# A two-layer hybrid encoder: the squares of the MLP norm taken unit by unit, one weight pool for all phases, and MLP weights prepared during the output projection

## Chip, cores and metric

One Trainium2 chip, one core, one launch. The metric is the device time of a run in microseconds (us); the median of three runs counts. A profile is one execution seen by the hardware profiler.

## The reference, cut to what matters

The input is 512 tokens of 1024 features; 16 learned tokens are put in front (L = 528). Two layers follow, each an attention block and an MLP, each behind an RMS norm, everything in float32:

```python
for layer in range(DEPTH):                       # DEPTH = 2
    u = rmsnorm(h, attn_norm_g[layer])
    mix = ab_mixer(...) if layer % 2 == 0 else c_mixer(...)   # both end in an output projection
    h = h + mix
    u = rmsnorm(h, mlp_norm_g[layer])            # u * rsqrt(mean(u*u) + 1e-6) * g
    h = h + square(relu(u @ w_ff1[layer])) @ w_ff2[layer]     # 1024 -> 4096 -> 1024
return h[:, N_META:]
```

The square of the ReLU lets the norm's factor be taken out: `r2` = 1 / (mean(h*h) + eps) is multiplied onto the MLP's result instead of onto its input.

## The kernel before, in words

Features lie on the 128 partitions, tokens along the free axis; `hk[m]` (m = 0 to 7) is the residual of feature tile m, 128 x 528. A float32 product is made of three reduced-precision ones: weights and activations are each split into a high part (a cast on ScalarE: `wh`, `ah`, `xh`) and a low part (a subtraction on VectorE: `wl`, `al`, `xl`), and the matmuls wh·xh, wh·xl, wl·xh are accumulated. `load_unit` (L213) loads a unit of weights with a transfer on SP's queue, casts it (L221) and subtracts (L222); `gemm` (L225, matmuls at L232) multiplies. One unit is 8 x 128 x 128 weights, 512 KB, and at 528 tokens 48 matmuls.

The program runs through phases: attention of layer 0 (AB), its output projection (O0), MLP 0 (M0), attention of layer 1 (C), its projection (O1, in two halves of the contraction), MLP 1 (M1). In layer 1 the MLP works on the last 512 tokens. The order of the attention phases is written out by hand (`ORDER`, `ORDER_C`); within it, and everywhere else, a planner at build time places the instructions of each engine by program order and by its own estimate of when operands and buffers are free. Buffers come from pools stacked at the left or the right of SBUF. A pool that is closed gives its memory to the next one, and a tile there waits for the tiles that lay in the same place. The weights of each phase have a pool of their own, opened by `weight_pool(name)`, which closes the one before (L155).

Output projection, layer 0 (L1159): for m = 0 to 7, load `hr` (the input tile) on SP's queue, multiply, add into `hk[m]` (L1164), `park(0, m)` it to device memory on POOL's queue (L1152), and call `fast.add(m)` (L1106). The last prepares the operands for the first MLP product, which is done with seven products of half size where eight would be needed (a Strassen-like scheme over two halves of the features and of the tokens). Tiles 0 to 3 need few operations ("light" in what follows: one cast, two splits); tiles 4 to 7 ("heavy") make the combinations T2, T3, T4 with tile m - 4. In O1 the same is done at L1510.

MLP (`mlp`, L1174): four quarters q of 1024 hidden features. In a quarter, four `pair` calls make 16 weight groups' worth of products (L1250, 336 matmuls), then eight units of the second weight matrix follow (L1318, 48 matmuls each, or 24 of double width in layer 1), whose results are gathered in `hk[m]`. `weight_groups` (L1196) prepares the groups one after the other: for a pair of first-matrix units it makes the four sums of half units with one add over 1024 elements (L1226) and two over 512 (L1228, L1230), then casts (L1201) and subtracts (L1202). `prepare` keeps a ring of five groups ahead of the products. The MLP's weight pool is opened when the MLP begins (L1177), on the left, where the temporaries of `fast` and the projection's weights were.

Sum of squares: after the products of quarter 1, `sum_squares` (L1136) reloads the eight parked tiles on POOL's queue (L1191, two `hr` buffers), squares each on ScalarE (L1143) and adds on VectorE (L1146). A matmul with the constant `onesd` (L1313) sums over the features, L1315 adds eps, L1316 takes the reciprocal `r2`. It is first used in quarter 2 (L1331).

Of the kernel before, what the change touches and what calls it, by code (L numbers as in the profile page):

```python
# [17 lines left out]
P = 128  # L18
D = 1024
KT = D // P  # L20
# [114 lines left out]
def build(tc, ins, out, dbg=None):  # L135
# [13 lines left out]
    cst = ctx.enter_context(tc.tile_pool(name="cst", bufs=1, side="left"))  # L149
    xp = ctx.enter_context(tc.tile_pool(name="xp", bufs=1, side="left"))  # L150
    dp = ctx.enter_context(tc.tile_pool(name="dp", bufs=1, space=DRAM))

    wpool = {}

    def weight_pool(name, bufs=2):  # L155

        if "cm" in wpool:
            wpool.pop("cm").__exit__(None, None, None)
        if name is not None:
            wpool["cm"] = tc.tile_pool(name=name, bufs=bufs, side="left", reuse_waits="tile")  # L160
            wpool["p"] = wpool["cm"].__enter__()
        return wpool["p"]

    weight_pool("wab")
# [48 lines left out]
    def load_unit(src):  # L213

        k, m = src.shape[1], src.shape[2]
        wp = wpool["p"]
# [824 lines left out]
    weight_pool(None)  # L1041
# [94 lines left out]
    def sum_squares(pool, src, tags=("sqk", "sqa")):  # L1136

        sq = None
        for k in range(KT):
            s = pool.tile([P, L], F32, name="sqk", tag=tags[0], bufs=2)  # L1140
            x = src(k)
            t0 = L - x.shape[1]
            S.activation(out=s[:, t0:], in_=x, func=AF.Square)  # L1143
            if k:
                t = pool.tile([P, L], F32, name="sqa", tag=tags[1], bufs=2)
                V.tensor_tensor(out=t[:, t0:], in0=sq[:, t0:], in1=s[:, t0:], op=ALU.add)  # L1146
                s = t
            sq = s
        return sq
# [3 lines left out]

    fq_cm = tc.tile_pool(name="fq0", bufs=1, side="left", reuse_waits="tile")
    fq = fq_cm.__enter__()
    ft_cm = tc.tile_pool(name="ft0", bufs=1, side="left", reuse_waits="tile")
    fast = Fast(fq, ft_cm.__enter__(), PK_G + 8, 0)
    weight_pool("wo0")
    for m in range(KT):  # L1159
# [7 lines left out]
    weight_pool(None)  # L1167
    ft_cm.__exit__(None, None, None)
    yp_cm.__exit__(None, None, None)
    tap("h1", h)  # L1170

    RING = 5

    def mlp(layer, t0, fast, final):  # L1174
        lp_cm = tc.tile_pool(name=f"mlp{layer}", bufs=1, side="right", reuse_waits="tile")
        lp = lp_cm.__enter__()
        wp = weight_pool(f"wm{layer}")  # L1177
# [15 lines left out]

        def weight_groups():  # L1196
            def split(src):
                k = src.shape[1]
                wh = wp.tile([P, KT, P], F32R, name="wh", tag="wh", bufs=RING)
                wl = wp.tile([P, KT, P], F32R, name="wl", tag="wl", bufs=RING)  # L1200
                S.copy(out=wh[:, :k], in_=src)  # L1201
                V.tensor_tensor(out=wl[:, :k], in0=src, in1=wh[:, :k], op=ALU.subtract)  # L1202
                return wh, wl

            def load(name, i):
                raw = wp.tile([P, 4, 4, P], F32, name="raw", tag="raw", bufs=2)
                for j in range(2):
                    nc.sync.dma_start(out=raw[:, 2 * j:2 * j + 2].rearrange("p a k m -> p (a k) m"),
                                      in_=ins[f"{name}_{layer}"][i + j])
                return raw  # L1210

            flat = lambda t: t.rearrange("p a k m -> p (a k) m")
            todo = [(w, q * 8 + m) for q in range(4) for w in ("w1", "w2") for m in range(0, 8, 2)]
            loaded = [load(*todo[0])]
            for i, (w, m) in enumerate(todo):
                if i + 1 < len(todo):
                    loaded.append(load(*todo[i + 1]))
                raw = loaded.pop(0)
                if w == "w2":
                    yield split(flat(raw[:, 0:2]))  # L1220
                    yield split(flat(raw[:, 2:4]))
                    continue
                s = wp.tile([P, 4, 4, P], F32, name="sums", tag="sums", bufs=1)
                yield split(flat(raw[:, 0:2]))
                wide4 = lambda t: t.rearrange("p a k m -> p a (k m)")
                V.tensor_tensor(out=wide4(s[:, 1:3]), in0=wide4(raw)[:, 0:4:3],  # L1226
                                in1=wide4(raw[:, 2:3]).to_broadcast([P, 2, 4 * P]), op=ALU.add)
                V.tensor_tensor(out=s[:, 3], in0=s[:, 2], in1=raw[:, 0], op=ALU.add)  # L1228
                yield split(flat(s[:, 2:4]))
                V.tensor_tensor(out=s[:, 0], in0=s[:, 3], in1=raw[:, 1], op=ALU.add)  # L1230
                yield split(flat(s[:, 0:2]))
                yield split(raw[:, 3])

        source = weight_groups()
        groups, used = [], set()

        def prepare():

            while len(groups) < RING or len(groups) - RING in used:
# [377 lines left out]
```

## Time and profile before

| | |
|---|---|
| median of 3 runs | 1378.26 us (1375.27 to 1379.09) |
| the profiled execution | 1378.83 us, span 1377.1 us |
| mean granted clock of TensorE | 0.967 of 2.4 GHz |
| VectorE, ScalarE, POOL busy | 67%, 51%, 8% of the span |
| DMA queues, share of 16 engines | SP's 22.7%, POOL's 2.9% |

The span is the time from the first to the last instruction. A matmul's record overlaps its neighbours', so a busy TensorE is not one at its peak; where it stands idle, the views name what ended the wait. Times within the span are us from its start. PEclk is the granted clock of TensorE as a share of 2.4 GHz; 0.5 means that it ran at 1.2 GHz.

### The profile page before, as it was taken

Reading aid. Unit: us, or ns where it says so; the run is one execution under the profiler, and the core shown is the slowest. Engines: PE = TensorE matmul, PEld = TensorE weight load, DVE = VectorE, ACT = ScalarE, POOL = GpSimd, SP = SyncE. Lnnn points to the kernel's source line nnn. Section 1 sums busy time; section 2 is a strip of 40 time slices with the busy share of each in tenths; the row PEclk is TensorE's granted clock in tenths of the full one; section 3 lists DMA queues with packets and bytes.
Section 4 is the critical chain, followed back from the end, with each engine's and each line's share of the span. In section 5 each row is a group of like instructions: output and inputs, shape, how many; then the busy total and the mean of one; then the engine's idle time right before and its main releaser. Section 6 shows DMA issues by size and latency. Waiting matters only on the chain.

```text
span 1377.1 us, 22737 instructions
## 1 busy us (share of the span) xinstructions
PE 1288.0 (94%) x8979; PEld 1188.1 (86%) x8979; DVE 921.8 (67%) x1847; ACT 702.0 (51%) x1412; POOL 113.7 (8%) x250
## 2 busy tenths in 40 slices
PE   7989998999879999599999999999989995999998
PEld 6988998888779999599999988888779894898996
DVE  6687769785568537547677468698786384476762
ACT  4634655566436538217347166675566372173460
POOL 1060505210010000100000000000100001000000
PEclk9998999999898999799999999999989997999999
DMA  4321211000453414312424011101334133124241
GB/s 165 108 62 31 63 32 47 1 2 14 142 158 106 138 47 134 113 63 92 154 78 168 32 47 47 44 19 34 127 138 148 61 128 117 62 95 151 78 138 46
DMA packets 35930, 118.08 MB, mean 86 GB/s; under 512 B 4456, under 2 KB 4584, under 8 KB 35696
## 3 DMA queue, kind: packets, MB, share of 16 engines
q1 hardware_dynamic: 31984, 103.86, 22.7%
q0 software_dynamic: 3840, 12.78, 2.9%
q8 instruction: 70, 1.15, 0.3%
q14 instruction: 36, 0.29, 0.1%
HBM read 110.25 MB, written 6.37 MB: 85 GB/s over the span
## 4 chain that ended last, share of the span: by engine, by line
PE 63%; issue 24%; DVE 5%; ACT 4%; POOL 2%; DMA 2%; SPq 0%; POOLq 0%; ACTq 0%; DVEq 0%
PE dn L232 28%; PE dn L1250 12%; PE cq L232 5%; PE po L1495 2%; PE dn L1468 2%; DMA hr<-hdram 1%; PE pw L1489 1%; PE pw L993 1%; POOL u L647 1%; DVE cy L442 1%; PE rw L695 1%; POOL ut L646 1%; PE rw L681 1%; PE rw L748 1%; PE rw L736 1%
## 5 line engine op out<-in xcount | busy, mean ns | idle before, releaser
L232 PE MATMUL dn<-ah,wh 128*128 128x264 f32 (+1 forms) x896 | 234.5, 320 | 4.9 <-ACT wh L221 4.9
L232 PE MATMUL dn<-ah,wl 128*128 128x264 f32 (+1 forms) x896 | 232.3, 318 | 0.6 <-DVE wl L222 0.6
L232 PE MATMUL dn<-al,wh 128*128 128x264 f32 (+1 forms) x896 | 231.3, 316 | 0.0
L1201 ACT CAST wh<-raw 128x1024 fp32r<-128x1024 f32 (+1 forms) x128 | 120.5, 943 | 201.1 <-PE dn L232 172.1
L1202 DVE TENSOR_TENSOR wl<-raw,wh 128x1024 fp32r<-128x1024 f32 (+1 forms) x128 | 139.3, 1090 | 63.9 <-ACT wh L1201 62.2
L232 PEld LDWEIGHTS dn<-ah,wh 128*128 128x128 f32 x896 | 149.6, 191 | 16.2 <-ACT wh L221 5.1
L1250 PE MATMUL dn<-xh,wh 128*128 128x264 f32 (+1 forms) x512 | 152.6, 298 | 11.7 <-ACT wh L1201 10.9
L232 PEld LDWEIGHTS dn<-al,wh 128*128 128x128 f32 x896 | 149.6, 191 | 12.0 <-issue 0.5
L232 PEld LDWEIGHTS dn<-ah,wl 128*128 128x128 f32 x896 | 148.6, 190 | 11.8 <-DVE wl L222 0.9
L1250 PE MATMUL dn<-xh,wl 128*128 128x264 f32 (+1 forms) x512 | 146.8, 289 | 1.6 <-DVE wl L1202 1.6
L1250 PE MATMUL dn<-xl,wh 128*128 128x264 f32 (+1 forms) x512 | 147.2, 288 | 0.0
L1250 PEld LDWEIGHTS dn<-xh,wh 128*128 128x128 f32 x512 | 99.2, 194 | 18.1 <-ACT wh L1201 12.1
L1202 DVE TENSOR_TENSOR wl<-sums,wh 128x1024 fp32r<-128x1024 f32 x64 | 78.0, 1224 | 39.4 <-ACT wh L1201 38.8
L1201 ACT CAST wh<-sums 128x1024 fp32r<-128x1024 f32 x64 | 66.8, 1050 | 72.4 <-PE dn L232 45.2
L1250 PEld LDWEIGHTS dn<-xh,wl 128*128 128x128 f32 x512 | 98.9, 194 | 2.5 <-DVE wl L1202 2.5
L1250 PEld LDWEIGHTS dn<-xl,wh 128*128 128x128 f32 x512 | 99.4, 194 | 0.1
L221 ACT CAST wh<-raw 128x1024 fp32r<-128x1024 f32 (+1 forms) x58 | 54.0, 932 | 88.2 <-PE dn L232 48.1
L232 PE MATMUL dn<-xh,wh 128*128 128x264 f32 x416 | 91.5, 297 | 1.1 <-DVE last L1335 0.8
L232 PE MATMUL dn<-xl,wh 128*128 128x264 f32 x416 | 90.4, 293 | 0.0
L232 PE MATMUL dn<-xh,wl 128*128 128x264 f32 x416 | 89.2, 293 | 0.0
L1328 DVE TENSOR_TENSOR h<-h,dn 128x528 f32<-128x528 f32 (+1 forms) x32 | 22.3, 696 | 76.3 <-PE dn L232 76.3
L222 DVE TENSOR_TENSOR wl<-raw,wh 128x1024 fp32r<-128x1024 f32 (+1 forms) x58 | 63.0, 1088 | 11.6 <-ACT wh L221 11.1
(507 smaller groups left out, 2978.5 us busy)
## 6 DMA issues: line engine op xcount, KB each, us to landing
raw<-in_w SPq DMA_DIRECT2D x128, 512.0 KB, 4.3
raw<-in_w_in SPq DMA_DIRECT2D x22, 512.0 KB, 3.6
raw<-in_w_c SPq DMA_DIRECT2D x12, 512.0 KB, 3.6
hr<-hdram POOLq DMA_DIRECT2D x16, 264.0 KB, 3.0
raw<-in_w_o SPq DMA_DIRECT2D x8, 512.0 KB, 4.5
raw<-in_w_o SPq DMA_DIRECT2D x16, 256.0 KB, 2.6
hr<-hdram POOLq DMA_DIRECT2D x16, 256.0 KB, 2.9
gcb<-gdram SPq DMA_DIRECT2D x8, 264.0 KB, 4.4
```

What stands on the lines that cost most here:

```text
L221: S.copy(out=wh, in_=raw)
L222: V.tensor_tensor(out=wl, in0=raw, in1=wh, op=ALU.subtract)
L232: T.matmul(o, a[:, k, :], b[k][:, sl], start=first and k == 0 and i == 0, stop=last and k == n - 1 and i == 2)
L442: V.scalar_tensor_tensor(out=y[:, a:a + n], in0=x[:, b:b + n], scalar=w(j), in1=y[:, a:a + n], op0=ALU.mult, op1=ALU.add)
L646: G.tensor_tensor(out=ut[:, :, :, :n], in0=arow, in1=ucol, op=ALU.mult)
L647: G.tensor_tensor(out=udst, in0=udst, in1=ut[:, :, :, :n], op=ALU.subtract)
L1201: S.copy(out=wh[:, :k], in_=src)
L1202: V.tensor_tensor(out=wl[:, :k], in0=src, in1=wh[:, :k], op=ALU.subtract)
L1250: T.matmul(o, a[:, half * 4 + k, :], b, start=start and k == 0 and i == 0, stop=k == 3 and i == 2, skip_group_check=not start)
L1328: V.tensor_tensor(out=tview(ak), in0=tview(ak), in1=pview(ps), op=ALU.add)
L1468: T.matmul(ps[:, s, :HL], a[:, sl], b[:, s * HL:(s + 1) * HL], start=i == 0, stop=i == 2)
L1495: T.matmul(po, a[:, kc, :], b, start=kc == 0 and i == 0, stop=kc == NC and i == 2)
```

## The change

1. `sum_squares` now handles one tile. In the MLP it is called in each of the eight units of quarter 0, behind the copy of the unit's result, and adds into one tile `sq`; after quarter 1's products only the `onesd` matmul, L1315 and L1316 are left. The statistics of layer 1's attention call it eight times in a row.
2. One weight pool `wp` (two buffers each of raw, high and low parts) is opened at the start, below the other left pools, and kept to the end; `load_unit` takes its buffers in all phases. The MLP gets a further pool, `wm0` or `wm1` (raw 2, high 3, low 3, sums 1), and its groups and raw tiles go in turn to this one and to `wp`.
3. The preparing of groups becomes a class `Weights` that is made before the output projection's last part. After every second tile of O0 and of the second half of O1, `prepare` is called with limits of 1, 2 and 3 groups, and after the eighth without one (so to five).
4. The projections take the tiles in the order 0, 4, 1, 5, 2, 6, 3, 7.
5. The four sums of a pair are four adds of 512 elements each, and the first pair loads the next one's units after its third group instead of at once.
6. `yp` is closed before the temporaries of `fast`, which move to the right side.

```diff
     cst = ctx.enter_context(tc.tile_pool(name="cst", bufs=1, side="left"))
+    wp = ctx.enter_context(tc.tile_pool(name="wp", bufs=2, side="left"))
     xp = ctx.enter_context(tc.tile_pool(name="xp", bufs=1, side="left"))
...
-    weight_pool("wab")
...
+    def sum_squares(pool, k, sq, x, tag="sqk"):
+        t0 = L - x.shape[1]
+        if k == 0:
+            S.activation(out=sq[:, t0:], in_=x, func=AF.Square)
+            return
+        s = pool.tile([P, L], F32, name="sqk", tag=tag, bufs=2)
+        S.activation(out=s[:, t0:], in_=x, func=AF.Square)
+        V.tensor_tensor(out=sq[:, t0:], in0=sq[:, t0:], in1=s[:, t0:], op=ALU.add)
...
+    RING = 5
+    class Weights:
+        def __init__(self, layer, pool):
+            self.layer, self.pool = layer, pool
+            self.groups, self.used, self.raws = [], set(), 0
+            self.source = self.produce()
+        def place(self, n, size, kind, dtype):
+            pool, bufs = (self.pool, size - 2) if n % size < size - 2 else (wp, 2)
+            return pool.tile([P, KT, P], dtype, name=kind, tag=kind, bufs=bufs)
+        def load(self, w, m):
+            o = []
+            for i in (m, m + 1):
+                o.append(self.place(self.raws, 4, "raw", F32))
+                self.raws += 1
+                nc.sync.dma_start(out=o[-1], in_=ins[f"{w}_{self.layer}"][i])
+            return o
+        def split(self, src):
+            k, n = src.shape[1], len(self.groups)
+            wh, wl = (self.place(n, RING, kind, F32R) for kind in ("wh", "wl"))
+            S.copy(out=wh[:, :k], in_=src)
+            V.tensor_tensor(out=wl[:, :k], in0=src, in1=wh[:, :k], op=ALU.subtract)
+            self.groups.append((wh, wl))
+        def produce(self):
+            todo = [(w, q * 8 + m) for q in range(4) for w in ("w1", "w2") for m in range(0, 8, 2)]
+            loaded = [self.load(*todo[0])]
+            for i, (w, m) in enumerate(todo):
+                ahead = lambda: loaded.append(self.load(*todo[i + 1])) if i + 1 < len(todo) else None
+                if i:
+                    ahead()
+                u0, u1 = loaded.pop(0)
+                if w == "w2":
+                    yield self.split(u0)
+                    yield self.split(u1)
+                    continue
+                s = self.pool.tile([P, 4, 4, P], F32, name="sums", tag="sums")
+                yield self.split(u0)
+                V.tensor_tensor(out=s[:, 2], in0=u1[:, :4], in1=u1[:, 4:], op=ALU.add)
+                V.tensor_tensor(out=s[:, 3], in0=s[:, 2], in1=u0[:, :4], op=ALU.add)
+                yield self.split(s[:, 2:4].rearrange("p a k m -> p (a k) m"))
+                V.tensor_tensor(out=s[:, 0], in0=s[:, 3], in1=u0[:, 4:], op=ALU.add)
+                V.tensor_tensor(out=s[:, 1], in0=u0[:, :4], in1=u1[:, :4], op=ALU.add)
+                yield self.split(s[:, 0:2].rearrange("p a k m -> p (a k) m"))
+                if not i:
+                    ahead()
+                yield self.split(u1[:, 4:])
+        def prepare(self, limit=None):
+            while len(self.groups) < RING or len(self.groups) - RING in self.used:
+                if limit is not None and len(self.groups) >= limit or next(self.source, self) is self:
+                    return
+
     fq_cm = tc.tile_pool(name="fq0", bufs=1, side="left", reuse_waits="tile")
     fq = fq_cm.__enter__()
-    ft_cm = tc.tile_pool(name="ft0", bufs=1, side="left", reuse_waits="tile")
+    wm_cm = tc.tile_pool(name="wm0", bufs=1, side="left", reuse_waits="tile")
+    weights = Weights(0, wm_cm.__enter__())
+    yp_cm.__exit__(None, None, None)
+    ft_cm = tc.tile_pool(name="ft0", bufs=1, side="right", reuse_waits="tile")
     fast = Fast(fq, ft_cm.__enter__(), PK_G + 8, 0)
-    weight_pool("wo0")
-    for m in range(KT):
+    MIXED = (0, 4, 1, 5, 2, 6, 3, 7)
+    for i, m in enumerate(MIXED):
...
         park(0, m)
         fast.add(m)
+        if i % 2:
+            weights.prepare((i + 1) // 2 if i < 7 else None)
...
             if q == 1:
-                sq = sum_squares(lp, reload, ("c0", "c1"))
                 ps = ps_dense()
...
                 if q == 0:
                     S.copy(out=tview(ak), in_=pview(ps))
+                    sum_squares(lp, m, sq, reload(m), "c0")
...
-        for m in range(KT):
+        for i, m in enumerate(MIXED):
             mark("O1")
-            ps = ps1("cq") if k0 == 0 else ps1(("cq", "po")[m % 2])
+            ps = ps1("cq") if k0 == 0 else ps1(("cq", "po")[i % 2])
...
                 fast.add(m)
+                if i % 2:
+                    weights.prepare((i + 1) // 2 if i < 7 else None)
...
+    wm_cm = tc.tile_pool(name="wm1", bufs=1, side="left", reuse_waits="tile")
+    weights = Weights(1, wm_cm.__enter__())
     weave((c_out(4, KT), 1))
```

## Rows read from the trace of the kernel before

**Rows 1.** The page's first part: busy us of each engine, its share of the span, its instructions.
```profile
PE 1288.0 (94%) x8979; PEld 1188.1 (86%) x8979; DVE 921.8 (67%) x1847; ACT 702.0 (51%) x1412; POOL 113.7 (8%) x250
```

**Rows 2.** The view of waits, TensorE's own: waiting tile and line, what released it, us in total, times, longest.
```profile
PE dn L1313 <- DVE sqa L1146: 33.6, 2, 16.9
PE dn L1250 <- ACT wh L1201: 10.9, 3, 6.5
...
PE dn L232 <- ACT wh L221: 4.9, 1, 4.9
PE po L232 <- DVE wl L222: 3.2, 1, 3.2
```

**Rows 3.** The timeline of POOL, ScalarE, VectorE and TensorE around the sum of squares of layer 0: start, duration (us), engine, line, operation, operands, count, and in brackets the idle time before and what ended it. One tile of the eight, and the matmul at the end.
```profile
557.05 0.55 POOL L1191 DMA_DIRECT2D hr<-hdram  x1 [1.48 <-ACT sqk L1143]
...
560.00 0.65 ACT L1143 ACTIVATE sqk<-hr 128x528 f32<-128x528 f32 x1 [1.42 <-DMA hr<-hdram]
...
560.68 0.71 DVE L1146 TENSOR_TENSOR sqa<-sqa,sqk 128x528 f32<-128x528 f32 x1 [1.35 <-ACT sqk L1143]
...
565.35 2.13 PE L1313 MATMUL dn<-sqa,onesd 128*128 128x264 f32 x4 [16.88 <-DVE sqa L1146]
```

**Rows 4.** The chain that ended last, in order of time: start, us, what. L232 here are the unit stages of the MLPs, L1250 their product stages, L1313 the `onesd` matmul of layer 1's MLP, L1362 the same four matmuls in layer 1's attention statistics.
```profile
615.65 42.60 PE dn L1250 x336
658.24 46.30 PE dn L232 x384
...
804.15 1.16 PE dn L1362 x4
...
1152.57 2.07 PE dn L1313 x2
...
1200.87 41.53 PE dn L1250 x336
1242.40 44.18 PE dn L232 x192
```

**Rows 5.** The groups of instructions by line: line, engine, operation, operands, count, busy us, mean ns of one, idle before and its releasers.
```profile
L1202 DVE TENSOR_TENSOR wl<-sums,wh 128x1024 fp32r<-128x1024 f32 x64 | 78.0, 1224 | 39.4 <-ACT wh L1201 38.8 <-PE dn L1250 0.5
...
L1226 DVE TENSOR_TENSOR sums<-raw 128x1024 f32<-128x1024 f32 x32 | 39.0, 1220 | 0.8 <-DMA raw<-in_w 0.6
...
L1230 DVE TENSOR_TENSOR sums<-sums,raw 128x512 f32<-128x512 f32 x32 | 22.1, 692 | 1.0
...
L1146 DVE TENSOR_TENSOR sqa<-sqa,sqk 128x528 f32<-128x528 f32 (+1 forms) x18 | 12.6, 703 | 15.1 <-ACT sqk L1143 14.7
...
L1143 ACT ACTIVATE sqk<-hr 128x528 f32<-128x528 f32 (+1 forms) x16 | 10.2, 638 | 15.9 <-DMA hr<-hdram 13.2 <-DVE sqa L1146 2.7
```

**Rows 6.** The timeline from O0 to M0, SP's queue and TensorE (columns as in rows 3): the first MLP loads, the last projection matmuls, the first product, the first product record of 0.28 us, the start of the unit stage.
```profile
406.30 3.44 SPq L1208 DMA_DIRECT2D raw<-in_w  x4
...
404.13 0.41 PE L232 MATMUL dn<-ah,wl 128*128 128x264 f32 x2
410.99 0.59 PE L1250 MATMUL dn<-xh,wh 128*128 128x264 f32 x1 [6.45 <-ACT wh L1201]
...
421.30 0.28 PE L1250 MATMUL dn<-xh,wh 128*128 128x264 f32 x1
...
459.51 0.41 PE L232 MATMUL dn<-ah,wh 128*128 128x264 f32 x2
```

**Rows 7.** Windows: from:to, length, then for PE, PEld, DVE, ACT and POOL busy us (instructions), granted clock, DMA share, GB/s. The first is O1, the second O0, the third the end of the attention of layer 0, the fourth the end of O1.
```profile
976.00:1003.70 27.70, 21.24 (x87) 16.36 (x85) 24.31 (x53) 17.53 (x34) 5.41 (x10) 0.90 0.58 192
353.20:404.50 51.30, 49.52 (x384) 49.04 (x384) 30.22 (x51) 19.74 (x33) 4.54 (x8) 0.94 0.46 136
300.00:349.50 49.50, 46.98 (x358) 41.67 (x356) 27.89 (x86) 31.81 (x105) 1.83 (x13) 1.00 0.10 33
992.00:1003.70 11.70, 5.24 (x18) 3.36 (x16) 10.63 (x26) 6.26 (x12) 1.62 (x3) 0.76 0.58 205
```

**Rows 8.** TensorE's timeline from O1 to M1: the second tile's first matmul, the wait for a low part in the last tile, the first product, the start of the unit stage.
```profile
976.40 0.39 PE L232 MATMUL po<-ah,wh 128*128 128x512 f32 x1
...
996.88 0.50 PE L232 MATMUL po<-ah,wl 128*128 128x512 f32 x1 [3.22 <-DVE wl L222]
...
1003.75 0.58 PE L1250 MATMUL dn<-xh,wh 128*128 128x256 f32 x1 [3.29 <-ACT wh L1201]
...
1050.08 0.40 PE L232 MATMUL dn<-ah,wh 128*128 128x512 f32 x1
```

**Rows 9.** Timelines of SP's queue, POOL, ScalarE, VectorE and TensorE at the start of O0: the last attention weights and the first projection weights loaded, a reload of quarter 1 issued in O0, the first activation casts, the weight casts, the last low parts of the activations, the first projection matmul.
```profile
211.17 0.33 SPq L220 DMA_DIRECT2D raw<-in_w_in  x1
...
342.49 0.33 SPq L220 DMA_DIRECT2D raw<-in_w_o  x1
...
400.31 0.55 POOL L1191 DMA_DIRECT2D hr<-hdram  x1
...
348.99 2.22 ACT L1067 CAST ah<-yA 128x528 fp32r<-128x528 f32 x4
...
353.25 1.99 ACT L221 CAST wh<-raw 128x1024 fp32r<-128x1024 f32 x2
...
352.48 2.56 DVE L1068 TENSOR_TENSOR al<-yB,ah 128x528 fp32r<-128x528 f32 x4
...
354.34 0.81 PE L232 MATMUL dn<-ah,wh 128*128 128x264 f32 x2 [4.88 <-ACT wh L221]
```

More of the change, by code (lines that the diff above doesn't have):

```diff
@@ L149, in build @@
     cst = ctx.enter_context(tc.tile_pool(name="cst", bufs=1, side="left"))
+    wp = ctx.enter_context(tc.tile_pool(name="wp", bufs=2, side="left"))
     xp = ctx.enter_context(tc.tile_pool(name="xp", bufs=1, side="left"))
     dp = ctx.enter_context(tc.tile_pool(name="dp", bufs=1, space=DRAM))
[L153 to L162, printed above, removed]
-    weight_pool("wab")
     psum = {}
@@ L215, in load_unit @@
         k, m = src.shape[1], src.shape[2]
-        wp = wpool["p"]
         raw = wp.tile([P, k, m], F32, name="raw", tag="raw")
@@ L1040, in build @@
     ab_cm.__exit__(None, None, None)
-    weight_pool(None)
     psum_pool("psm0", dn=4)
@@ L1134, in add @@
             self.split("T4", i, *part("T4"), t4, -1.0)
[L1136 to L1149, printed above, removed]
+    def sum_squares(pool, k, sq, x, tag="sqk"):
[6 more added lines that the diff above has]
+        V.tensor_tensor(out=sq[:, t0:], in0=sq[:, t0:], in1=s[:, t0:], op=ALU.add)
@@ L1166, in build, with mlp @@
         fast.add(m)
-    weight_pool(None)
+        if i % 2:
+            weights.prepare((i + 1) // 2 if i < 7 else None)
     ft_cm.__exit__(None, None, None)
-    yp_cm.__exit__(None, None, None)
     tap("h1", h)
-    RING = 5
-    def mlp(layer, t0, fast, final):
+    def mlp(layer, t0, fast, weights, final):
         lp_cm = tc.tile_pool(name=f"mlp{layer}", bufs=1, side="right", reuse_waits="tile")
         lp = lp_cm.__enter__()
-        wp = weight_pool(f"wm{layer}")
+        groups, used, prepare = weights.groups, weights.used, weights.prepare
         n = fast.n
@@ L1192, in reload @@
             return o
[L1196 to L1239, printed above, removed]
-                g = next(source, None)
-                if g is None:
-                    return
-                groups.append(g)
         def product(o, g, half, name, start):
@@ L1301, in mlp @@
         r2, base = None, 0
+        sq = lp.tile([P, L], F32, name="sqa")
         for q in range(4):
@@ L1341, in build @@
     xs2 = []
-    mlp(0, 0, fast, lambda m: xs2.append(make_x(m, PK_G + 16)))
-    weight_pool(None)
+    mlp(0, 0, fast, weights, lambda m: xs2.append(make_x(m, PK_G + 16)))
+    wm_cm.__exit__(None, None, None)
     fq_cm.__exit__(None, None, None)
@@ L1350, in build @@
     psum_pool("psc", dn=2, pw=2, po=1, cq=1)
-    weight_pool("wc")
     cp_cm = tc.tile_pool(name="cp", bufs=1, side="right", reuse_waits="tile")
@@ L1358, in stats @@
     def stats():
-        sq = sum_squares(cp, lambda k: hk[k])
+        sq = cp.tile([P, L], F32, name="sqa", tag="sqa")
+        for k in range(KT):
+            sum_squares(cp, k, sq, hk[k])
         ps = ps_dense()
@@ L1529, in build @@
     fast = Fast(fq, ft_cm.__enter__(), PK_G + 24, NM)
+    wm_cm = tc.tile_pool(name="wm1", bufs=1, side="left", reuse_waits="tile")
+    weights = Weights(1, wm_cm.__enter__())
     weave((c_out(4, KT), 1))
     ft_cm.__exit__(None, None, None)
-    weight_pool(None)
     tap("h3", h)
@@ L1536, in build @@
     mark("M1")
-    mlp(1, NM, fast, lambda m: nc.sync.dma_start(out=out[m], in_=hk[m][:, NM:]))
-    weight_pool(None)
+    mlp(1, NM, fast, weights, lambda m: nc.sync.dma_start(out=out[m], in_=hk[m][:, NM:]))
+    wm_cm.__exit__(None, None, None)
     fq_cm.__exit__(None, None, None)
```

## The prediction

> **What bounds the kernel now.** I read the page's busy times first: TensorE is busy for 94% of the span [rows 1], so a gain must come from the stretches where it stands still or runs at its lower clock. The view of waits on TensorE lists them: of the larger ones, one line takes 33.6 us in two waits, the `onesd` matmul of L1313 behind the sum of squares; then come three waits of the first MLP products for their prepared weights (10.9 us), the first output projection waiting for its weight cast (4.9), and an output-projection product of layer 1 waiting for VectorE (3.2) [rows 2]. The timeline around the first long wait shows why it lasts: a reload is issued only when the square before last has freed one of two `hr` buffers, the square waits for the transfer, the add for the square, about 1.9 us a tile, and TensorE starts after the eighth [rows 3]. All four kinds of wait are touched by the change.
>
> **Sum of squares: the price per layer.** TensorE did its last product before the wait at 565.35 - 16.88 = 548.47 us [rows 3], and the unit stage of that quarter ended where the next products begin, at 615.65: 67.2 us. The same stage of the next quarter, without the wait, takes 46.30 us [rows 4]. What stays between is the `onesd` matmul alone; the same four matmuls of the layer-1 statistics, at full clock, take 1.16 us [rows 4]. So the stage becomes 46.30 + 1.16 = 47.5 and 19.7 us go. Layer 1: the wait is 33.6 - 16.9 = 16.7 us and ended at 1152.57, the stage at 1200.87: 1200.87 - (1152.57 - 16.7) = 65.0 us; the next quarter takes 44.18; with 1.1 us for the matmul 45.3, and 19.7 us go [rows 2, 4]. Both include the lower clock after the wait. Together **39.4 us**. What is late next is the reciprocal for `r2`, but it stays behind the same matmul on VectorE as before and its first user is a quarter later.
>
> The work moves into the eight units of the first quarter: per unit one reload on POOL's queue, one square (0.64 us on ScalarE) and one add (0.70 on VectorE) [rows 5]. A unit lasts 46.30/8 = 5.8 us on TensorE [rows 4], in which VectorE and ScalarE otherwise do about one weight split and one copy, so I cost it at nothing. The square stands on ScalarE behind the unit's PSUM copy and in front of the next group's cast; five groups are ready ahead, so a late reload would have to last several units before TensorE sees it. Uncovered it would cost 8 x (0.64 + 0.70) = 10.7 us a layer. The layer-1 attention statistics use the same helper with the same counts: nothing.
>
> **Sums of the first weights.** One add of 1024 elements (1220 ns) and two of 512 (692) become four of 512: 0.16 us more for each of 32 pairs, 5 us of VectorE in all [rows 5]. In the steady quarters VectorE has room, so nothing; 5 us if that cover were gone.
>
> **First weights in layer 0.** Today the loads for the MLP begin at 406.30, after the last projection matmul (404.13 + 0.41 = 404.54); the first product starts at 410.99, and the clock is back at the rate of 0.28 us per record only at 421.30. The unit stage begins at 459.51 [rows 6]. A stage of the same 336 matmuls takes 42.60 us when nothing is late [rows 4], so 459.51 - 404.54 - 42.60 = 12.4 us are lost. In the change groups 0 to 2 are ready inside the projection. That brings forward about 4 x 0.69 of sums and 4 x 1.22 + 0.68 of low parts, 8.4 us of VectorE (five groups), into a stage where it is busy 30.2 of 51.3 us [rows 5, 7]: it fits. The reordering 0, 4, 1, 5, ... matters here because a light tile (0 to 3) then follows each heavy one. The last tile, 7, is last in both orders, and its operands come 2 to 3 us after its matmul, while the first product (tiles 0 to 3 only) and three quarters of the second cover them. Groups 3 and 4 lie in the shared buffers and are split only after tile 7; group 4 is wanted after 60 products, about 7.3 us after the projection, and I expect it at 7. I take **10 us** of the 12.4, bounds 6 and 12.4.
>
> **First weights of the output projection, layer 0.** The pool kept through the phases has free raw, high and low buffers long before the projection: the last attention weights were issued at 211.17, the first projection weights only at 342.49, and their casts stand behind the eight activation casts, so TensorE begins at 354.34 after 4.88 us [rows 9]. The planner does move independent work far ahead: it issued a reload of the second quarter at 400.31 [rows 9], inside the projection, because its buffer was free. If it does so here, the two casts leave the start of the stage; TensorE is then paced by the low parts of the activations, which end at 352.48 + 2.56 = 355.0 [rows 9], and the first tile ends near 355.6 instead of about 404.5 - 7 x 5.8 = 364 (5.8 us being a unit of as many matmuls, 46.30/8 [rows 4]). Bounds: 0 (the casts stay) and 8; I take **5**, nearer to the upper one, since the moved reload is the nearest row. On the way the casts cost 2 x 2.3 us of ScalarE and VectorE in the attention stage, where TensorE is busy 47.0 of 49.5 us [rows 7]: bounds 0 and 4.5, I take 0.
>
> **First weights in layer 1.** Here VectorE is already the limit: 24.3 of 27.7 us from 976 on, 10.63 of the last 11.7 [rows 7]; TensorE waits 3.22 us for it before 996.88, waits 3.29 for the first weight cast before 1003.75, and the unit stage begins at 1050.08 [rows 8]. The second tile begins at 976.40 [rows 8]; seven tiles of 12 matmuls (44.18/16 = 2.76 us each) and a product stage of 41.53 [rows 4] would end at 976.4 + 19.3 + 41.5 = 1037.2, so 12.9 us are lost. But VectorE's work for the tiles has to be done before the second product can end, and groups 0 to 2 now add 4 x 0.69 + 3 x 1.22 = 6.4 us in front of tile 7. The 24.3 us of tile work plus 6.4, less some 2 for the last operands of tile 7 that are wanted later, end near 1006 if VectorE never idles, say 1006 to 1009; of the products, 336 - 21 then remain, 38.9 us: 1045 to 1048 before any slow clock. I take **2 us**, bounds -2 and +9 (the upper one if the groups can be prepared before the projection, which needs their memory to be free while the attention runs).
>
> **Sum.** 39.4 + 10 + 5 + 2 = 56.4. The rows come from one execution of 1378.8 us (span 1377.1, 1.7 around it), 0.6 above the median of the three runs, so nothing has to be shifted: 1378.8 - 56.4 = **1322 us**.
>
> **Rivals.** *Only the sum of squares pays* (15%): the early weights don't come early, because the loads' memory is held by the attention's tiles or VectorE is full, and what is won at the start of the MLP was lost in the projection. For it: layer 1's rows above. Against it: VectorE's 21 idle us in layer 0. 1378.8 - 39.4 = 1339, with the layer-0 bound 1333 to 1341.
> *All of it pays* (17%): 39.4 + 12.4 + 8 + 9 = 68.8, 1310 us. For it: the planner's reach. Against it: groups 3 and 4 come last, layer 1's VectorE.
> *The squares get in the way* (3%): the reload or the square of each unit holds ScalarE and the ring runs dry; with the uncovered 10.7 us in both layers the forecast becomes 1322 + 21 = 1343. Against it: the five groups ahead.
> *Slower* (2%): in the reordered projections VectorE is late once in every pair of tiles, and TensorE never gets back to 2.4 GHz. The stretch with the wait of 3.22 us was granted 0.76 [rows 7], and after the wait of 6.45 us the records stayed longer than 0.28 us, at 1.2 GHz, from 410.99 to 421.30 [rows 6]. In layer 1, at half the clock, the 96 projection matmuls and the 336 products would take up to twice as long, 22 + 41.5 = 64 us more, against 39.4 won: 1403 us. It decides from 39.4 + 17 us on, so only when nearly all of both stages runs at the lower clock. Against it: a stage limited by VectorE hides much of a slower TensorE.
> The Trainium skill, TensorE: Matmul & The Clock Gate, section HAM oscillation — how this bites in real kernels, says that a wait which returns in each pass of a loop drops the clock in each pass, so that the price is paid again and again instead of once. By that rule the last rival would be the forecast for layer 1; the trace agrees as far as single waits go (the 0.76 above), and no row shows waits that return.
>
> **How the numbers follow.** The forecast has 60%, the rest is small mixtures of these. Its own range is 1315 to 1330 from the bounds of its terms. The range for 8 in 10 takes in the case in which all pays and most of that in which only the sum of squares does: 1307 to 1341. About 0.3% (4 us) is what a measurement of this kernel can tell from no change; of the cases only the slower one and a sliver of the mixtures reach it, so faster 0.96, the same 0.01, slower 0.03.
>
> **What would show it.** Right: no wait of TensorE at the `onesd` matmul and a second-quarter unit stage near 47.5 and 45.3 us; squares one per unit in the first quarter; in layer 0 the unit stage beginning some 43 to 46 us after the last projection matmul; the first projection casts before the activation casts. In layer 1 I expect TensorE's waits for VectorE inside the projection to grow and those after it to shrink. Wrong: a wait at `onesd` that is still several us, waits of the units in the first quarter, or a projection stage of layer 0 clearly longer than 8 x 5.8 us.

## The result, and the profile after

The changed kernel takes 1324.27 us (median of four runs, 1323.57 to 1325.03), the kernel before beside it 1378.67 (1375.27 to 1380.79): a ratio of 0.9608, 95% interval 0.9587 to 0.9628. The forecast was 1322. The span went from 1377.1 to 1322.8 us, 54.3 less. On the page TensorE is now busy for 97% of it instead of 94 [rows 1], and its mean granted clock is 0.988 instead of 0.967.

The busy times of the page, and TensorE's longer waits (what waited, for what, us in total, times, longest):

```profile
PE 1279.5 (97%) x8979; PEld 1181.8 (89%) x8979; DVE 917.9 (69%) x1879; ACT 699.3 (53%) x1412; POOL 114.5 (9%) x250
```

```profile
PE cq L220 <- DVE h L1508: 4.2, 2, 2.7
PE dn L1246 <- DVE wl L1167: 3.3, 2, 1.9
...
PE dn L1360 <- DVE sqa L1131: 1.4, 1, 1.4
```

Of the four kinds of wait in [rows 2] only the last has a successor of its size: in O1 TensorE now waits 4.2 us for the adds into `h`. The 33.6 us at the `onesd` matmul (now L1309) are gone.

The chain that ended last (start, us, what) has the stages in order. L220 are the units of 48 matmuls (before: L232), L1246 the products (before: L1250); the lines answer to [rows 4]:

```profile
442.55 46.33 PE dn L220 x384
...
579.04 42.78 PE dn L1246 x336
621.83 46.31 PE dn L220 x384
...
1014.37 44.16 PE dn L220 x192
...
1145.67 42.01 PE dn L1246 x336
1187.69 44.14 PE dn L220 x192
```

Four starts and the end, held against those of before, say where the time went. The first unit stage of MLP 0 begins 17.0 us earlier (442.55 for 459.51), that of the third quarter 36.4 earlier (621.83 for 658.24); in layer 1 the first begins 35.7 earlier (1014.37 for 1050.08), the third 54.7 earlier (1187.69 for 1242.40), and the end is 54.3 earlier. So the start of layer 0 gives 17.0, each sum of squares some 19, layer 1's start nothing (-0.6).

The timeline around the squares, to be read against [rows 3] (start, us, engine, line, operands; idle time before in brackets):

```profile
403.15 0.66 ACT L1127 ACTIVATE sqa<-hr 128x528 f32<-128x528 f32 x1
437.84 0.66 ACT L1130 ACTIVATE sqk<-hr 128x528 f32<-128x528 f32 x1
...
455.37 0.65 ACT L1130 ACTIVATE sqk<-hr 128x528 f32<-128x528 f32 x1 [2.05 <-DMA hr<-hdram]
...
531.45 1.05 PE L1309 MATMUL dn<-sqa,onesd 128*128 128x264 f32 x4
...
1100.40 1.02 PE L1309 MATMUL dn<-sqa,onesd 128*128 128x512 f32 x2
```

The two `onesd` matmuls carry no bracket: no wait. The first square runs at 403.15, before the first unit, and the last at 455.37, when two of the eight units are done. They don't come one per unit, as the prediction had it: nothing ties a square to its unit, and the planner ran them ahead.

The start and the end of O0, against [rows 6, 9]:

```profile
234.99 1.03 ACT L209 CAST wh<-raw 128x1024 fp32r<-128x1024 f32 x1
...
348.88 2.22 ACT L1054 CAST ah<-yA 128x528 fp32r<-128x528 f32 x4
349.55 1.46 PE L220 MATMUL dn<-ah,wh 128*128 128x264 f32 x4
...
353.14 1.05 ACT L1166 CAST wh<-raw 128x1024 fp32r<-128x1024 f32 x1
...
398.40 0.40 PE L220 MATMUL dn<-ah,wl 128*128 128x264 f32 x2
398.65 0.28 PE L1246 MATMUL dn<-xh,wh 128*128 128x264 f32 x1
```

The first weight cast of the projection (L209) now runs at 234.99, far inside the attention, and TensorE begins 0.67 us after the first activation cast starts instead of 5.35; the first MLP group is cast at 353.14; and the first product follows the last projection matmul without a gap, with records of 0.28 us from the first one on, where before came a wait of 6.45 and 10 us of longer records [rows 6]. The granted clock from 398.3 to 442.5 is 1.00.

O1 is the stage that did not gain. TensorE's timeline, against [rows 8]:

```profile
947.95 0.47 PE L220 MATMUL cq<-ah,wh 128*128 128x512 f32 x1 [1.50 <-DVE h L1508]
...
958.40 0.47 PE L220 MATMUL cq<-ah,wh 128*128 128x512 f32 x1 [2.71 <-DVE h L1508]
...
970.14 0.39 PE L1246 MATMUL dn<-xh,wh 128*128 128x256 f32 x1 [0.96 <-ACT xh L1086]
...
974.93 0.38 PE L1246 MATMUL dn<-xh,wl 128*128 128x256 f32 x1 [1.86 <-DVE wl L1167]
```

The waits of 3.22 and 3.29 us of before are replaced by these four, 7.0 us in all. Below, "the stretch" is the time from the start of the last unit stage of MLP 0 to that of the first of MLP 1. It took 1050.08 - 747.17 = 302.9 us before and 1014.37 - 710.91 = 303.5 after.

### The profile page after: what moved, and what is told of

Read it like the earlier page. It is cut to its first block, busy times and chain, and to the rows that moved or that the text cites. A ratio compares the mean times of both kernels' runs of the same rounds, so it can differ in the third digit from the quotient of the medians.

```text
span 1322.8 us, 22818 instructions
## 1 busy us (share of the span) xinstructions
PE 1279.5 (97%) x8979; PEld 1181.8 (89%) x8979; DVE 917.9 (69%) x1879; ACT 699.3 (53%) x1412; POOL 114.5 (9%) x250
## 4 chain that ended last, share of the span: by engine, by line
PE 85%; DVE 6%; ACT 4%; POOL 2%; issue 1%; DMA 1%; SPq 0%; ACTq 0%; DVEq 0%
PE dn L220 37%; PE dn L1246 25%; PE cq L220 5%; PE po L1493 2%; PE dn L1466 2%; PE pw L981 1%; PE pw L1487 1%; POOL u L635 1%; DVE cy L430 1%; POOL ut L634 1%; PE po L220 1%; PE rw L736 1%; PE rw L669 1%; PE rw L683 1%; PE pw L465 1%
## 5 line engine op out<-in xcount | busy, mean ns | idle before, releaser
L220 PE MATMUL dn<-ah,wh 128*128 128x264 f32 (+1 forms) x896 | 232.1, 318 | 0.0
L220 PE MATMUL dn<-ah,wl 128*128 128x264 f32 (+1 forms) x896 | 230.3, 316 | 0.0
L220 PE MATMUL dn<-al,wh 128*128 128x264 f32 (+1 forms) x896 | 229.6, 314 | 0.0
L1167 DVE TENSOR_TENSOR wl<-raw,wh 128x1024 fp32r<-128x1024 f32 (+1 forms) x128 | 139.4, 1089 | 41.0 <-ACT wh L1166 39.4
L220 PEld LDWEIGHTS dn<-al,wh 128*128 128x128 f32 x896 | 148.3, 189 | 11.6 <-issue 0.2
L220 PEld LDWEIGHTS dn<-ah,wh 128*128 128x128 f32 x896 | 148.0, 190 | 10.8 <-ACT ah L1054 0.3
L220 PEld LDWEIGHTS dn<-ah,wl 128*128 128x128 f32 x896 | 147.1, 189 | 11.0
L1246 PE MATMUL dn<-xh,wh 128*128 128x264 f32 (+1 forms) x512 | 150.1, 294 | 1.0 <-ACT xh L1086 1.0
L1246 PE MATMUL dn<-xh,wl 128*128 128x264 f32 (+1 forms) x512 | 144.8, 284 | 3.3 <-DVE wl L1167 3.3
L1246 PE MATMUL dn<-xl,wh 128*128 128x264 f32 (+1 forms) x512 | 145.3, 285 | 0.1
L1246 PEld LDWEIGHTS dn<-xh,wh 128*128 128x128 f32 x512 | 97.1, 190 | 7.2 <-ACT e L1266 3.7
L1246 PEld LDWEIGHTS dn<-xh,wl 128*128 128x128 f32 x512 | 97.1, 190 | 3.7 <-DVE wl L1167 3.7
L209 ACT CAST wh<-raw 128x1024 fp32r<-128x1024 f32 (+1 forms) x58 | 53.9, 929 | 87.2 <-PE dn L220 46.6
L1246 PEld LDWEIGHTS dn<-xl,wh 128*128 128x128 f32 x512 | 97.1, 190 | 0.7 <-DVE xl L1088 0.5
L220 PE MATMUL dn<-xh,wh 128*128 128x264 f32 x416 | 92.2, 299 | 0.2 <-ACT cin L432 0.2
L220 PE MATMUL dn<-xl,wh 128*128 128x264 f32 x416 | 90.8, 294 | 0.0
L220 PE MATMUL dn<-xh,wl 128*128 128x264 f32 x416 | 89.6, 294 | 0.0
```

Source lines behind the costliest of these rows:

```text
L220: T.matmul(o, a[:, k, :], b[k][:, sl], start=first and k == 0 and i == 0, stop=last and k == n - 1 and i == 2)
L1246: T.matmul(o, a[:, half * 4 + k, :], b, start=start and k == 0 and i == 0, stop=k == 3 and i == 2, skip_group_check=not start)
```

## The experiments

Each ran beside the kernel before; ratios are to it, with a 95% interval. The changed kernel's interval is 0.9587 to 0.9628. Starts, stages and stretches are read from one profiled execution each. The changed kernel and the two runs that leave layer 1's projection as it is ("the squares put back" and "the first unit of O0 apart") have stretches of 303.5, 302.4 and 302.6, the kernel before and "the squares alone" 302.9 and 304.45; so a difference of 1.5 us in a stretch says nothing.

**The squares alone.** The kernel before with `sum_squares` of the change and nothing else.

> The kernel before with part 1 of the change alone. Theory A (the four gains are independent, the squares are worth 39.4 us): 1378.7 - 39.4 = 1339 us, the unit stages of quarter 1 near 47.5 us in layer 0 and 45.3 in layer 1, no wait of TensorE at the onesd matmul, the unit stages of quarter 0 as they were (46.3 and 44.2). Rival B (in the changed kernel the squares are hidden only because the new pools give the ring more room; in the old layout the quarter-0 units are held up): 1345 to 1360, with waits of TensorE in the units of quarter 0.

1341.3 us, 0.9733 (0.9709 to 0.9756). The chain:

```profile
460.62 46.30 PE dn L232 x384
...
639.43 46.30 PE dn L232 x384
...
1032.76 44.18 PE dn L232 x192
...
1205.15 44.38 PE dn L232 x192
```

Against [rows 4, 6, 8] the first start is 1.1 us later and the third quarter's 18.8 earlier, 19.9 gained; in layer 1 from 17.3 to 37.2 earlier, again 19.9. The squares are worth 39.8 us by themselves, as A said; the time is 2.3 above A's 1339, because 1.1 and 1.5 us went at the two starts. In layer 0 the first square now stands on ScalarE, at 404.09, in front of a cast of the last tile. In layer 1 ScalarE and VectorE have the order of the kernel before up to the first product, so the 1.5 us are what one and the same order varies by; the granted clock in the 18 us behind the projection was 0.72 for 0.79. B falls: no unit waits.

**The squares put back.**

```diff
-                    sum_squares(lp, m, sq, reload(m), "c0")
...
             if q == 1:
+                for k in range(KT):
+                    sum_squares(lp, k, sq, reload(k), "c0")
```

> The changed kernel with the eight squares put back behind the products of quarter 1. Theory A: 1324.3 + 39.2 = 1363.5 us, with two waits of TensorE at the onesd matmul of about 16.8 us each and unit stages of 67 and 65 us. Rival B: less than 30 us come back, so some of what the stage of quarter 1 gained came with the new weight pools.

1354.5 us, 0.9835 (0.9814 to 0.9855): 30 us came back, not 39. TensorE waits less than in [rows 3]:

```profile
541.09 0.81 PE L1311 MATMUL dn<-sqa,onesd 128*128 128x264 f32 x1 [12.75 <-DVE sqa L1131]
```

The number is near B's, but its reason isn't shown by this: here too the first squares ran ahead, three of them before the products ended at 528.34, where before it was one, so fewer rounds of reload, square and add were left. It is a shorter chain, not that of before; what the squares are worth is told by the run before this. (The trace is of the fastest of four executions, 1350.94 us.)

**Without the calls of prepare.** Both calls inside the projections left out.

> The changed kernel without the calls of prepare inside the two projections; the pools stay where they are and the first groups are prepared at the start of the MLP by program order. Theory A (the calls bring the weights forward): in layer 0 the unit stage again begins about 55 us after the last projection matmul instead of 43.7, so 1324.3 + 11.3 = 1335.6 us. Rival C (the place of the pool does it: its memory is free early, and the planner moves the loads and casts forward by itself): 1323 to 1327 us, with the first cast of an MLP group still right behind the activation casts of layer 0.

1325.05 us, 0.9612 (0.959 to 0.9634), as the changed kernel; the first unit stage of MLP 0 begins at 442.89. C holds: the calls do nothing that the planner wouldn't. What brings the weights forward is the place of the pool, whose memory is free early.

**The pools opened late.** `wm0` and `wm1` opened after the projections in the memory of the temporaries of `fast`, no calls.

> The changed kernel with the MLP's own pools opened only after the projections, in the memory of the temporaries of fast, and without the calls. Layer 0: the groups cannot be made before the last heavy tile, so the 11.3 us are lost again, the unit stage beginning 52 to 56 us after the last projection matmul. Layer 1: theory D (VectorE is the limit there, so early groups win nothing): the unit stage of quarter 0 within 2 us of where it now lies; rival E (early groups pay there too, and the order of the tiles took the gain away): 4 us or more later. In all 1334 to 1338 us by D, 1340 or more by E.

1340.1 us, 0.9729 (0.9709 to 0.975).

```profile
349.19 49.13 PE dn L220 x384
453.15 46.33 PE dn L220 x384
...
721.49 46.36 PE dn L220 x384
...
1029.01 44.67 PE dn L220 x192
```

Layer 0: the unit stage begins 453.15 - 398.32 = 54.8 us after the projection, as before the change (55.0) instead of 43.7. That is the 11.3 us, and with the run above it shows that they hang on the pool's place. Layer 1: a stretch of 307.5, 4.1 longer than in the changed kernel, which speaks for E; but in the kernel before it was 302.9 with late weights as well. Three more runs ask for the difference.

**The natural order.** `MIXED` set to 0 to 7.

> The changed kernel with the tiles of both projections in the order 0 to 7. The run with late pools showed that early groups are worth 4.1 us in layer 1 (its unit stage of quarter 0 at 1029.01, with 10.6 us of that from layer 0), while from before to after nothing was won there; something else in the change took it. Theory F (the mixed order did: each heavy tile now stands in front of a light one and TensorE waits for the adds into h): in layer 1 the unit stage of quarter 0 comes 3 to 5 us earlier than 1014.4 less what layer 0 shifts. Rival G (the mixed order helps, because four heavy tiles in a row leave VectorE behind at the end; what was lost lies in the groups' own work): 2 to 6 us later. Layer 0, where VectorE has room: within 2 us of 442.6 by both. In all 1320 to 1323 by F, 1326 to 1333 by G.

1323.2 us, 0.9599 (0.9578 to 0.962): no difference that can be measured, and a stretch of 1012.65 - 709.20 = 303.45. F and G both fall. The order of the tiles neither took a gain nor gave one. With late pools in the same place and the natural order:

> The changed kernel with the MLP's pools opened only after the projections, as in the run with late pools, and with the tiles in the order 0 to 7. From the start of the last unit stage of MLP 0 to the first unit stage of MLP 1 it took 302.9 us in the kernel before, 303.5 in the changed one, 303.45 in the changed one with the order 0 to 7, and 307.5 with late pools and the mixed order. If late groups cost the same in either order: 307 us again, 1339 to 1341 in all. If the mixed order is what makes late groups dear: 303 us, as before, and 1334 to 1337.

1343.1 us, 0.9739 (0.9714 to 0.9765), with a stretch of 1030.00 - 718.47 = 311.5, longer still and expected by neither side. So the place in those temporaries is a bad one in itself, and a run with the place of before was needed:

> The changed kernel with the order 0 to 7, the second half of layer 1's projection on weight buffers of its own, and the MLP's pool of layer 1 opened over those buffers afterwards, as the kernel before had it; on VectorE the sums of the first pair come behind the last heavy tile. If early groups win nothing in layer 1 (the work of VectorE is the same, only its order changes): the stretch from the last unit stage of MLP 0 to the first of MLP 1, 303.5 us, becomes 302.5 to 304.5 and the time 1322 to 1325. If they win 4 us or more, as the two runs with pools in the memory of the temporaries seemed to say: 307 or more, 1327 and up.

1325.6 us, 0.9618 (0.9604 to 0.9631).

```profile
710.10 46.36 PE dn L219 x384
...
1017.17 44.16 PE dn L219 x192
```

The stretch is 307.1, the second answer, but it is read from the slowest of five executions (1323.43 to 1327.36 us), and by its time this kernel can't be told from the changed one. The sums stand behind the last heavy tile on VectorE, as in the kernel before, but the placing is not the same: the first MLP group is cast 259.3 us into the stretch, there at 255.5, and TensorE waits 4.57 us for a low part where it waited 3.22 [rows 8]. Late weights thus give stretches from 302.9 to 311.5, early ones 302.4 to 303.8: early groups beat the late versions tried here, but not the one that the kernel before had.

What early groups do shows on VectorE. Its last operand for the projection's tiles is the low part of T4 of tile 7; after and then before:

```profile
974.79 0.41 DVE L1090 SCALAR_TENSOR_TENSOR T4l<-t,T4h 128x256 fp32r<-128x256 f32 x1
```

```profile
1005.09 0.42 DVE L1103 SCALAR_TENSOR_TENSOR T4l<-t,T4h 128x256 fp32r<-128x256 f32 x1
```

After, it ends 264.3 us into the stretch, and the unit stage begins 39.2 us later; before, it ends at 258.3, and the unit stage begins 44.6 later. Early groups put their work in front of this operand, late ones behind it, and the sum is nearly the same. The 39.2 returns in the natural order and without the calls, and 44.9 to 46.8 in the three runs with late pools. In those three the operand ended at 262.1 to 264.8, later than in the kernel before though no group stands in front of it; that is most of what makes them slower than it, and which detail of their placing delays the tiles stays open.

**Less and more for VectorE.** In the first run `load_unit` returns the high part twice for the second half of O1; in the second the line of `xl` for heavy tiles of layer 1 is executed three times.

> The changed kernel without the low parts of the weights in the second half of layer 1's projection (the high parts are multiplied in their place, as many matmuls; this leaves out part of the computation): eight subtractions of 0.69 us, 5.5 us, less for VectorE, nothing else. Theory D (VectorE's whole work in the projection decides when the MLP can begin): the stretch of 303.5 us becomes 298 to 300, the time 1319 to 1321. Rival L (a chain of casts and adds from tile to tile decides, with VectorE idle between): less than 1.5 us, 1323 to 1325.

> The changed kernel with the low part of each heavy tile in layer 1's projection computed three times instead of once: 4 x 2 x 0.75 = 6 us more for VectorE. Theory D: the stretch of 303.5 us becomes 308 to 309.5, the time 1329 to 1330. Rival L: less than 2 us more, 1324 to 1326.

1317.8 us, 0.9571 (0.9538 to 0.9605), and 1327.6 us, 0.963 (0.9609 to 0.9652). The chains of the two, the first with less work:

```profile
707.30 46.36 PE dn L222 x384
...
1004.89 44.16 PE dn L222 x192
```

```profile
709.81 46.36 PE dn L220 x384
...
1017.73 44.16 PE dn L220 x192
```

With 5.5 us less the stretch is 297.6, 5.9 shorter; with 6.0 more it is 307.9, 4.5 longer. The times of the first, 1315.08 to 1322.78, lie all below those of the changed kernel, the times of the second, 1327.28 to 1327.96, all above. The first trace is of the fastest of its four executions. D's numbers were missed by a little on both sides, but the direction and size are D's, and L falls: in O1 the amount of VectorE's work decides when the MLP can begin. The last T4 operand moved with it, to 260.0 and 268.8 us into the stretch; another 1.6 us of the first run lie behind that operand, where the granted clock was also higher (0.96 for 0.91 in the 18 us behind the projection).

**The first unit of O0 apart.**

```diff
-    def load_unit(src):
+    def load_unit(src, pool=None):
...
-        raw = wp.tile([P, k, m], F32, name="raw", tag="raw")
+        raw = (pool or wp).tile([P, k, m], F32, name="raw", tag="raw")
...
+    wo_cm = tc.tile_pool(name="wo0", bufs=1, side="left", reuse_waits="tile")
+    wo = wo_cm.__enter__()
...
-        gemm(full(ps), load_unit(ins["w_o0"][m]), yh, yl)
+        gemm(full(ps), load_unit(ins["w_o0"][m], None if i else wo), yh, yl)
```

> The changed kernel with the raw tile of the first unit of layer 0's projection in a buffer of its own on top of the left pools, memory that the attention still holds for most of its time; so its load cannot come before the end of the attention. Theory H (the 5.7 us at the start of the projection came from casts that no longer stand behind the activation casts): the casts fall back behind the eight activation casts, TensorE waits for the first one some 4 to 5 us, and the time becomes 1328 to 1330 us. Rival I (the start was won elsewhere, in the order of the attention's last steps): 1323 to 1326 us.

1330.4 us, 0.9643 (0.9628 to 0.9659). The timeline at the start of O0:

```profile
352.01 2.21 ACT L1054 CAST ah<-yA 128x528 fp32r<-128x528 f32 x4
...
356.26 1.99 ACT L209 CAST wh<-raw 128x1024 fp32r<-128x1024 f32 x2
357.35 0.81 PE L220 MATMUL dn<-ah,wh 128*128 128x264 f32 x2 [4.87 <-ACT wh L209]
```

H holds: the wait of [rows 9] is back, 4.87 for 4.88. Of the 7.8 us by which TensorE starts later than in the changed kernel, 3.1 come earlier, from an attention that ends later; why it ends later was not traced.

**The sums on POOL**, meant to relieve VectorE (`G` for `V` in the four adds):

> The changed kernel with the four sums of each pair of weight units on POOL instead of VectorE, 2.7 us less for VectorE per pair. In the kernel before, POOL took about 1.27 us for an operation on 128x512. Theory J (VectorE is what limits layer 1's projection and what lengthened the product stages by 0.15 and 0.48 us): the unit stage of quarter 0 in layer 1 comes 1.5 to 3 us earlier, the product stages go back to 42.6 and 41.5, together 3 to 5 us: 1319 to 1322. Rival K (POOL's adds are late or hold up VectorE): waits of TensorE for the casts of the sums in the product stages, 1326 us or more. Between them, 1323 to 1325, VectorE was not the limit.

1343.9 us, 0.9746 (0.9732 to 0.9761): 20 us slower than the changed kernel. J falls; K's time came, by its second reason, POOL holding up VectorE, for TensorE's longer new waits are for low parts (8.3 us in two waits) and not for casts of the sums. Layer 0's first unit stage begins 4.0 us later, the stretch is 11.6 longer, and the six later product stages take 0.6 more each. VectorE and POOL in the product stage of the last quarter:

```profile
1260.52 1.80 DVE L1167 TENSOR_TENSOR wl<-raw,wh 128x512 fp32r<-128x512 f32 x1 [0.16 <-ACT wh L1166]
1262.51 1.51 DVE L1253 TENSOR_TENSOR al<-c,ah 128x512 fp32r<-128x512 f32 x1 [0.19 <-ACT ah L1252]
1263.94 0.41 DVE L1269 TENSOR_TENSOR c<-e,dn 128x256 f32<-128x256 f32 x1
...
1260.48 1.29 POOL L1188 TENSOR_TENSOR sums<-raw 128x512 f32<-128x512 f32 x1
1261.72 1.75 POOL L1185 TENSOR_TENSOR sums<-sums,raw 128x512 f32<-128x512 f32 x1
1263.55 1.62 POOL L1187 TENSOR_TENSOR sums<-sums,raw 128x512 f32<-128x512 f32 x1
```

A subtraction of 512 elements, 0.69 us elsewhere, takes 1.80 and 1.51 beside a POOL add; the add with an operand in PSUM (L1269) keeps its 0.41. The Trainium skill, SBUF — State Buffer, section SBUF: two separate sides, says that VectorE's operations with two SBUF inputs and GpSimd's share a port pair that the one who comes first holds for a whole instruction; these lines agree. In O1, where VectorE is the limit, the stretch grew to 315.1.

**Two units in one buffer.** One cast and one subtraction for two half units in the second half of O1.

> The changed kernel with the half units of the second half of layer 1's projection loaded two to a buffer, one cast and one subtraction for both: 4 x (2 x 0.69 - 1.22) = 0.6 us less for VectorE in all, and two more of the low parts are ready before the stage, 1.4 us. Theory D: 1 to 2 us less, 1322 to 1323. Rival M (the casts of a pair wait for two transfers and stand in front of the first tile's work): 1325 us or more.

1326.0 us, 0.9618 (0.9593 to 0.9643), a stretch of 305.2. The median is M's, but the runs (1323.58 to 1328.21) overlap with those of the changed kernel: what is shown is that nothing was won. The view of waits has a wait of the kind that M named, for the low part of a pair in the projection:

```profile
PE cq L231 <- DVE wl L221: 6.0, 1, 6.0
```

## Why the prediction came out right

The order of the steps is that of the prediction.

- *Sum of squares, 39.4.* The stage of quarter 1 in layer 0 runs from 531.45 to 579.04, 47.6 us (47.5 predicted, 67.2 before); in layer 1 from 1100.40 to 1145.67, 45.3 (45.3, 65.0). That is 39.3 us won, and the run of this part alone shows 39.8. The hidden work cost nothing: the unit stages of quarter 0 kept 46.33 and 44.16. Only the picture was wrong: the squares ran ahead of the units.
- *First weights in layer 0, 10.* Measured 55.0 - 43.7 = 11.3, inside 6 to 12.4. The stage is within 1.1 us of 42.60. The change gave the early work to the calls of `prepare`; the runs show that the place of the pool does it.
- *First weights of O0, 5.* Measured 5.7 at the projection's end (398.83 for 404.54), and the casts left the start of the stage as forecast. What paces the first tile is another thing than forecast: the low parts of the activations end at 355.1, as it said, but the tile's result is added only at 358.5 instead of near 355.6, for TensorE had a granted clock of 0.50 from 349.5 to 354.5. That the choice of 5 between 0 and 8 came out is in part luck.
- *First weights in layer 1, 2.* Measured -0.6, inside -2 to 9, and the step that was mis-sized. The mechanism is the one forecast: VectorE's work ends, and the products that are then left take the rest, 38.9 us in the forecast and 39.2 in the trace. The added and the subtracted work show that the limit is real. What was mis-sized is VectorE's end: 264.3 us into the stretch is 1011.5 on the time axis of the kernel before, not 1006 to 1009. From the second tile on the forecast added up 28.7 us of work; the trace has 32.1 us busy and 3.0 idle up to that operand, with five groups' work in front of it and not three. The sign that was given for TensorE came in part: its waits inside the projection grew from 3.2 to 4.2 us and all those behind it shrank from 4.8 to 2.8, but of these the ones for VectorE alone grew, from 0.7 to 1.9. The projection now ends 3.9 us later (257.2 us into the stretch for 253.3), which uses up the wait of 3.29 for the first cast. The upper bound of 9 asked for groups made before the projection; SP issues their first loads only at 934.47, right behind a projection load that had waited 3.4 us for a weight buffer. Whether the pool's memory or the order of SP's queue held them is not shown.
- *Not priced.* The later product stages grew, from 42.60 to 42.78 in layer 0 and from 41.53 to 42.01 in layer 1, 1.8 us over six of them. The sums were costed at nothing, for VectorE had room. It has (31.1 busy of the 42.0 us from 1145.67); what changed is ScalarE's order at a change of pairs, to be seen in the two timelines, after and then before:

```profile
1156.21 0.63 ACT L1250 ACTIVATE c<-c 128x512 f32<-128x512 f32 x1
1156.75 0.35 ACT L1266 COPY e<-dn 128x256 f32<-128x256 f32 x1
...
1157.16 0.38 PE L1246 MATMUL dn<-xh,wh 128*128 128x256 f32 x1
```

```profile
1211.77 0.36 ACT L1270 COPY e<-dn 128x256 f32<-128x256 f32 x1
1212.02 0.64 ACT L1254 ACTIVATE c<-c 128x512 f32<-128x512 f32 x1
...
1212.23 0.33 PE L1250 MATMUL dn<-xh,wh 128*128 128x256 f32 x1
```

After, a copy out of PSUM stands behind a square, and TensorE's next matmul begins just after its end (1157.10), 0.25 us after the one in front of it; before, it was 0.11. The 0.5 us of this stage gather between 11 and 29 us into it, in such small steps at the first two of its three changes of pairs and at the T2 product behind each; the third change is alike in both. That the sums' new form brought this order is argued, not tried. The runs narrow it: with the squares alone these stages took 42.5 and 41.6 us, as before, and without the calls, with late pools or in the natural order 42.7 and 42.0, as after. So neither the squares nor the calls, the late or early place or the order of the tiles made it; the form of the sums and the groups' turn between two pools are left.

The gain is 2.1 us smaller than forecast (54.3 for 56.4). The terms say +1.3 and +0.7 in layer 0, -0.1 in the squares, -2.6 in layer 1's start and -1.8 in the product stages, together -2.5; so the total is near in part because misses of both signs cancel. Of the rivals, "only the sum of squares pays" fell by layer 0's 17.0 us, "all of it pays" by layer 1, the uncovered squares by their unit stages. The slower one had its condition met in part (waits of 1.50 and 2.71 us once in a pair of tiles, granted clock 0.88 from 940 to 967.5), but the stretch is limited by VectorE, which hides nearly all of it: behind VectorE's last operand TensorE needed 39.2 us where the forecast had 38.9.

## What to carry to other kernels

A wait of a tensor engine behind a chain of small steps on other engines is worth its whole length if the steps can move to a stage where those engines have room; price it as this stage against its twin without the wait. Early work helps where the engine that does it is idle, and only moves the waits where that engine is the limit: ask for each stage which engine's sum ends last. And with a planner that runs ahead, it is the place of a buffer, not the place of a call, that decides when work starts.

## What was not expected of the hardware

VectorE's two-input subtractions of 512 elements took 1.5 to 1.8 us instead of 0.69 while POOL added, so moving the sums to POOL, 2.7 us of VectorE's work a pair, cost 20 us. And TensorE, kept busy from the projection into the MLP, held a granted clock of 1.00 from 398.3 to 442.5, where in the kernel before, after a wait of 6.45 us, the records stayed longer until 421.30 [rows 6] and the granted clock was 0.53 from 411 to 422.
